# A two-layer encoder on one core: branch B's conversions get a higher priority, and GpSimd makes some low parts of the output weights

## The chip, the cores and the metric

The kernel runs on one core of a Trainium2 chip. A core has five engines with queues of their own: TensorE (PE, matrix multiplications into PSUM), VectorE (DVE), ScalarE (ACT), GpSimd (POOL) and SyncE (SP, which here issues every DMA). The metric is the device time of one execution in microseconds.

## The reference

Two layers act on x, 512 positions by 1024 features in float32. Each layer is a half-step SwiGLU FFN, a token mixing with two branches of heads, and a second half-step FFN; every sub-layer is RMS-normed and modulated by a shift, a scale and a gate that come from a conditioning vector. This change touches the mixing alone:

```python
def token_mixing(h, cos, sin, w_in, sink, onorm_a, onorm_b, w_out):
    proj = h @ w_in
    qa, ka, va, qb, kb, vb = jnp.split(proj, IN_SPLITS, axis=-1)
    ...
    oa, _ = banded_attention(qa, ka, va, A_HALF_WINDOW, sink)
    for window, dilation in B_BRANCHES:
        o, l = dilated_branch(qb, kb, vb, window, dilation)
        ...
    wts = jax.nn.softmax(jnp.stack(lses, axis=0), axis=0)
    ob = jnp.sum(wts[..., None] * jnp.stack(outs, axis=0).astype(jnp.float32), axis=0).astype(h.dtype)
    ya = rmsnorm(oa.reshape(b, s, A_WIDTH), onorm_a)
    yb = rmsnorm(ob.reshape(b, s, B_WIDTH), onorm_b)
    return jnp.concatenate([ya, yb], axis=-1) @ w_out
```

Both branches have eight query heads of 64 features; q and k are turned by rope first, and branch A's eight heads share two of k and v.

## The kernel before

Activations lie transposed, features on the 128 partitions and the 512 positions along a row. To keep float32's precision, a matrix product is made of three: each operand is split into a high part (a copy in TensorE's own float32 format) and a low part (what the copy left out), and `mm3` (L224) adds high x high (L226), high x the weight's low (L227) and low x high (L228) in PSUM.

Weights come in chunks of 128x1024. `emit_chunk` (L139) issues the DMA of one into a tile `raw` (L153); ScalarE copies it to `hi` (L157) and VectorE subtracts to get `lo` (L158). For chunks near a change of sub-layer (`finer`) both are done in two pieces of 512 columns. The list `specs` holds the chunks in the order of use; a mixer ends with eight of `w_out`, four for branch B's half of the features (`half` 1), then four for branch A's.

The mixer makes q, k and v, then sixteen heads, B's eight first. One head: scores on TensorE (L698, L699), the mask and the row's least value on VectorE (L703, reading PSUM), exp on ScalarE (L707), a transpose of the probabilities on TensorE (`ptr`, L732), their high part on ScalarE (`ph`, L735) and low part on VectorE (`pl`, L736), and the product with v (`po`, L739, L740). The `rope` of each q and k tile uses VectorE and, for one product and for the low part, GpSimd (L612, L616); its results are copied into place by DMAs that SP issues.

`weave` interleaves the heads with a filling stream: after each step of a head it adds the rate of `RATES` to a debt and emits fill until the debt is paid. The fill is first the remaining projections (`fill_b`), then branch B's part of the output projection (`fill_a`): eight output tiles of four `mm3`, 96 matmuls. For that B's eight heads are normed: `stat` and `bcast` (L778, L787) are hooked into the tenth and eleventh heads, `bcast` ends in the tile R (L794), and `conv` (L796) scales each of B's four tiles by R (L800), makes its high part `yh` (L801) and its low part `yl` (L802). After the last head the rest of the fill is emitted, with branch A's norm, then A's four conversions (`yah`, `yal`) and A's part of the projection.

The order on each engine is fixed when the kernel is built. A scheduler takes the emitted instructions by priority, which is the place of emission unless `high_priority(offset=...)` moves it forward. Heads of branch B stand HB = 50 forward, those of A HA = 150, branch A's norm and conversions HP = 300. Branch B's conversions stand where they are emitted.

Of the kernel before, what the change touches and what calls it, by code (L numbers as in the profile page):

```python
# [11 lines left out]
F32 = mybir.dt.float32  # L12
# [3 lines left out]
ALU = mybir.AluOpType  # L16
# [29 lines left out]
HP = 300  # L46
# [6 lines left out]
VK = ((0, 3), (3, 3), (6, 2))  # L53
PAIRS = ("b0", "b1", "b2", "b3", "a0", "a1", "a2", "a3")
HJ = [(9, 0), (10, 0)]
RATES = ((0, 2.2), (4, 1.0), (8, 0.65))
HL = 200
BY_POOL = (1, 3, 4, 6, 7)
AW = 1.5
# [9 lines left out]
def tile_trunk(ctx: ExitStack, tc: tile.TileContext, xT, c, positions, adaT, cols, sink, wi1, wo1,  # L69
# [38 lines left out]
    temps = [None, None]  # L108
    specs = []
    finer = set()  # L110
    live = {}
    state = {"emit": 0, "use": 0}

    for l in range(L):
        for sub, (wi, wo) in enumerate(((wi1, wo1), (None, None), (wi2, wo2))):
            finer.update(range(len(specs) - 3, len(specs) + 6))
            if wi is None:
                specs += [wqk[l, QK.index(t)] for t in FIRST]
                for t in FILL:
                    if t[0] == "v":  # L120
                        for k0, n in VK:
                            specs.append(wv[l, int(t[1])][:, k0 * 320:(k0 + n) * 320])
                    else:
                        specs.append(wqk[l, QK.index(t)])
                for half in (1, 0):
                    for m2 in range(4):
                        specs.append(w_out[l, half, m2])
            else:
                for f0, n in THIRDS:
                    for f in range(f0, f0 + n):  # L130
                        if paired(l, sub, f):
                            specs.append((wi[l, f, 0], wi[l, f, 1]))
                        else:
                            specs.append(wi[l, f, 0])
                            specs.append(wi[l, f, 1])
                    for m in range(KD):
                        specs.append(wo[l, m][:, f0 * 128:(f0 + n) * 128])

    def emit_chunk(pieces=1):  # L139
        i = state["emit"]  # L140
# [10 lines left out]
        hi = wp.tile([128, 1024], F32R, tag="hi", name="hi")  # L151
        lo = wp.tile([128, 1024], F32R, tag="lo", name="lo")
        nc.sync.dma_start(raw[:, :n], ap)  # L153
        step = 512 if i in finer else n
        for a in range(0, n, step):
            sl = slice(a, min(a + step, n))
            A.activation(hi[:, sl], raw[:, sl], AF.Copy)  # L157
            V.tensor_tensor(lo[:, sl], raw[:, sl], hi.bitcast(F32)[:, sl], op=ALU.subtract)  # L158
        live[i] = (hi, lo)

    def parts(t):
# [435 lines left out]
    def mixer(l, norm, pool, mod):  # L597
# [313 lines left out]
        def fill_a():  # L911
            while not hasattr(bb, "R"):
                yield None
            for ft in range(4):
                bb.conv(ft)
                yield FT
            for job in jobs():
                m, W, w0 = job()
# [273 lines left out]
```

## Time and profile before

| | us |
|---|---|
| median of 3 runs (lowest, highest) | 1941.79 (1940.43, 1943.55) |
| profiled execution | 1941.13 |
| span of its profile | 1939.4 |
| TensorE busy | 1903.8 (98%) |
| VectorE busy | 1516.0 (78%) |
| ScalarE busy | 941.6 (49%) |
| GpSimd busy | 85.5 (4%) |

The profile is one execution. The span runs from its first instruction to its last; the execution has 1.7 us around it. A matmul's duration overlaps the next one's, so TensorE can be busy and yet not at its pace; the number of matmuls in a stretch says more. The heads of the first mixer end shortly before 610 us of the span, those of the second shortly before 1550.

### The profile page before, as it was taken

The numbers are of one execution on the slowest core, as the hardware profiler recorded it, in microseconds if no ns is written. First come the engines' busy times: TensorE is split into PE (matmuls) and PEld (weight loads), VectorE is DVE, ScalarE is ACT, GpSimd is POOL, SyncE is SP. The second block draws the span as 40 slices with busy tenths as digits, with TensorE's granted clock in tenths as the row PEclk, the third lists the DMA queues.
The fourth block names the chain that finished last, engine by engine and source line by source line (L and its number), as shares of the span: only waits on it lengthen the run. The fifth ranks groups of instructions, "written<-read, shape, count | busy, mean of one in ns | idle before, by whom it ended". The sixth has DMA issues, their size and how long they took to land.

```text
span 1939.4 us, 30969 instructions
## 1 busy us (share of the span) xinstructions
PE 1903.8 (98%) x12000; PEld 1711.2 (88%) x12000; DVE 1516.0 (78%) x2653; ACT 941.6 (49%) x1782; POOL 85.5 (4%) x63
## 2 busy tenths in 40 slices
PE   7999999999999999999999999999999999999998
PEld 5788888898778999989999898999887799898998
DVE  8967484477888989899688898867778889686873
ACT  5422222246675554536445363644567656363552
POOL 2000000011210000000000000000211000000000
PEclk8999999999999999999999999999999999999999
DMA  8778384245422255464424545342543113233231
GB/s 298 282 255 308 126 304 137 76 129 139 118 55 66 77 164 195 142 209 129 142 66 152 196 144 161 109 131 83 153 116 99 44 57 111 86 106 123 87 110 44
DMA packets 84677, 267.95 MB, mean 138 GB/s; under 512 B 10673, under 2 KB 13361, under 8 KB 84530
## 3 DMA queue, kind: packets, MB, share of 16 engines
q1 hardware_dynamic: 84530, 265.98, 42.6%
q8 instruction: 94, 1.54, 0.3%
q14 instruction: 53, 0.43, 0.1%
HBM read 244.97 MB, written 2.10 MB: 127 GB/s over the span
## 4 chain that ended last, share of the span: by engine, by line
PE 90%; DVE 5%; ACT 2%; DMA 2%; issue 1%; SPq 0%; POOL 0%; DVEq 0%; ACTq 0%; POOLq 0%
PE mm L226 17%; PE mm L227 17%; PE mm L228 17%; PE mm L488 10%; PE mm L489 10%; PE mm L490 10%; PE ptr L732 2%; PE po L739 1%; PE po L740 1%; PE s L698 1%; PE s L699 1%; DVE araw L320 1%; DMA araw<-in_adaT_dram 1%; PE mm L661 1%; PE mm L663 1%
## 5 line engine op out<-in xcount | busy, mean ns | idle before, releaser
L157 ACT ACTIVATE hi<-raw 128x512 fp32r<-128x512 f32 (+5 forms) x253 | 215.7, 866 | 310.2 <-PE mm L228 224.2
L158 DVE TENSOR_TENSOR lo<-raw,hi 128x512 fp32r<-128x512 f32 (+5 forms) x253 | 259.2, 1037 | 88.6 <-ACT hi L157 87.6
L226 PE MATMUL mm<-hh,hi 128*128 128x512 f32 (+1 forms) x864 | 307.7, 357 | 6.9 <-ACT hh L298 6.6
L228 PE MATMUL mm<-hl,hi 128*128 128x512 f32 (+1 forms) x864 | 303.1, 355 | 2.8 <-DVE hl L299 2.8
L227 PE MATMUL mm<-hh,lo 128*128 128x512 f32 (+1 forms) x864 | 305.8, 355 | 0.0
L227 PE MATMUL mm<-gh,lo 128*128 128x512 f32 (+1 forms) x832 | 297.0, 357 | 0.0
L226 PE MATMUL mm<-gh,hi 128*128 128x512 f32 (+1 forms) x832 | 296.8, 357 | 0.0
L228 PE MATMUL mm<-gl,hi 128*128 128x512 f32 (+1 forms) x832 | 296.5, 356 | 0.0
L488 PE MATMUL mm<-sh,hi 128*128 128x256 f32 x912 | 260.0, 285 | 0.3 <-ACT sc L518 0.3
L489 PE MATMUL mm<-sh,lo 128*128 128x256 f32 x912 | 258.1, 283 | 0.0
L490 PE MATMUL mm<-sl,hi 128*128 128x256 f32 x912 | 258.0, 283 | 0.0
L185 ACT ACTIVATE hi<-raw 128x512 fp32r<-128x512 f32 x228 | 132.0, 623 | 140.3 <-issue 73.6
L396 DVE SCALAR_TENSOR_TENSOR x<-mm,fin,x 128x512 f32<-128x512 f32 (+1 forms) x156 | 101.4, 653 | 115.7 <-PE mm L228 115.2
L226 PEld LDWEIGHTS mm<-hh,hi 128*128 128x128 f32 x864 | 164.6, 191 | 29.7 <-ACT hh L298 8.1
L228 PEld LDWEIGHTS mm<-hl,hi 128*128 128x128 f32 x864 | 163.2, 190 | 25.9 <-DVE hl L299 4.7
L227 PEld LDWEIGHTS mm<-hh,lo 128*128 128x128 f32 x864 | 164.4, 190 | 20.7 <-DVE lo L1004 0.3
L228 PEld LDWEIGHTS mm<-gl,hi 128*128 128x128 f32 x832 | 157.2, 189 | 22.7
L227 PEld LDWEIGHTS mm<-gh,lo 128*128 128x128 f32 x832 | 157.2, 189 | 22.3
L226 PEld LDWEIGHTS mm<-gh,hi 128*128 128x128 f32 x832 | 157.2, 189 | 22.2
L488 PEld LDWEIGHTS mm<-sh,hi 128*128 128x128 f32 x912 | 174.0, 191 | 0.7 <-ACT sc L518 0.6
L489 PEld LDWEIGHTS mm<-sh,lo 128*128 128x128 f32 x912 | 174.2, 191 | 0.0
L490 PEld LDWEIGHTS mm<-sl,hi 128*128 128x128 f32 x912 | 174.1, 191 | 0.0
(185 smaller groups left out, 4017.1 us busy)
## 6 DMA issues: line engine op xcount, KB each, us to landing
raw<-in_wi_dram SPq DMA_DIRECT2D x171, 512.0 KB, 3.7
araw<-in_adaT_dram SPq DMA_DIRECT2D x144, 512.0 KB, 4.6
raw<-in_wo_dram SPq DMA_DIRECT2D x64, 448.0 KB, 3.8
raw<-in_wo_dram SPq DMA_DIRECT2D x32, 512.0 KB, 3.6
raw<-in_wqk_dram SPq DMA_DIRECT2D x26, 512.0 KB, 3.7
raw<-in_w_out_dram SPq DMA_DIRECT2D x16, 512.0 KB, 3.7
kh<-qh SPq DMA_DIRECT2D x40, 128.0 KB, 2.3
kl<-t SPq DMA_DIRECT2D x40, 128.0 KB, 2.3
```

What stands on the lines that cost most here:

```text
L157: A.activation(hi[:, sl], raw[:, sl], AF.Copy)
L158: V.tensor_tensor(lo[:, sl], raw[:, sl], hi.bitcast(F32)[:, sl], op=ALU.subtract)
L185: A.activation(d, r, AF.Copy)
L226: T.matmul(ps, wh, X[0][:, s], start=start, stop=False)
L227: T.matmul(ps, wl, X[0][:, s], start=False, stop=False)
L228: T.matmul(ps, wh, X[1][:, s], start=False, stop=stop)
L320: return V.tensor_tensor_reduce(out=raw, in0=raw, in1=by, scale=1.0, scalar=0.0, op0=ALU.mult, op1=ALU.add, accum_out=mod[:, l, ch, k:k + ...
L396: ins = V.scalar_tensor_tensor(x[:, m, s], ps[:, s], gate[:, m:m + 1], x[:, m, s], op0=ALU.mult, op1=ALU.add).ins
L488: T.matmul(ps, wh, xh, start=start and k == 0, stop=False, skip_group_check=True)
L489: T.matmul(ps, wl, xh, start=False, stop=False, skip_group_check=True)
L490: T.matmul(ps, wh, xl, start=False, stop=stop and k == 3, skip_group_check=True)
L732: T.transpose(p[:, j * 128:j * 128 + 128], self.sm[qt][:, c0:c0 + 128], ident)
```

## The change

Three things. The rate of filling from the ninth head on (branch A's heads) goes from 0.65 to 0.55. Four of each mixer's eight `w_out` chunks, the third to the sixth in the list, are split in pieces of 512, and their subtraction is issued on GpSimd in place of VectorE. And branch B's four conversions are emitted with the priority HP.

```diff
--- before.py
+++ after.py
@@ -53,7 +53,7 @@
 VK = ((0, 3), (3, 3), (6, 2))
 PAIRS = ("b0", "b1", "b2", "b3", "a0", "a1", "a2", "a3")
 HJ = [(9, 0), (10, 0)]
-RATES = ((0, 2.2), (4, 1.0), (8, 0.65))
+RATES = ((0, 2.2), (4, 1.0), (8, 0.55))
 HL = 200
 BY_POOL = (1, 3, 4, 6, 7)
 AW = 1.5
@@ -108,6 +108,7 @@
     temps = [None, None]
     specs = []
     finer = set()
+    by_pool = set()
     live = {}
     state = {"emit": 0, "use": 0}
 
@@ -124,6 +125,8 @@
                         specs.append(wqk[l, QK.index(t)])
                 for half in (1, 0):
                     for m2 in range(4):
+                        if m2 // 2 == half:
+                            by_pool.add(len(specs))
                         specs.append(w_out[l, half, m2])
             else:
                 for f0, n in THIRDS:
@@ -151,11 +154,11 @@
         hi = wp.tile([128, 1024], F32R, tag="hi", name="hi")
         lo = wp.tile([128, 1024], F32R, tag="lo", name="lo")
         nc.sync.dma_start(raw[:, :n], ap)
-        step = 512 if i in finer else n
+        step = 512 if i in finer or i in by_pool else n
         for a in range(0, n, step):
             sl = slice(a, min(a + step, n))
             A.activation(hi[:, sl], raw[:, sl], AF.Copy)
-            V.tensor_tensor(lo[:, sl], raw[:, sl], hi.bitcast(F32)[:, sl], op=ALU.subtract)
+            (G if i in by_pool else V).tensor_tensor(lo[:, sl], raw[:, sl], hi.bitcast(F32)[:, sl], op=ALU.subtract)
         live[i] = (hi, lo)
 
     def parts(t):
@@ -912,7 +915,8 @@
             while not hasattr(bb, "R"):
                 yield None
             for ft in range(4):
-                bb.conv(ft)
+                with tc.high_priority(offset=HP):
+                    bb.conv(ft)
                 yield FT
             for job in jobs():
                 m, W, w0 = job()
```

VectorE's order at branch B's conversions in the first mixer. Before (L715 and L716 make a head's denominator, L755 and L750 a head's result, L611 and L613 belong to a rope, L703 and L736 as above):

```order
L611 TENSOR_TENSOR t_4802<-mm,rc 128x512
L715 TENSOR_TENSOR den<-den,es 128x4
L800 SCALAR_TENSOR_TENSOR y<-y,col,R 128x512
L716 RECIPROCAL den<-den 128x4
L613 TENSOR_TENSOR t_4802<-t_4802,part 128x512
L800 SCALAR_TENSOR_TENSOR y<-y,col,R 128x512
L802 TENSOR_TENSOR yl<-y,yh 128x512
L736 TENSOR_TENSOR pl<-ptr,ph 128x384
L736 TENSOR_TENSOR pl<-ptr,ph 128x256
L802 TENSOR_TENSOR yl<-y,yh 128x512
L800 SCALAR_TENSOR_TENSOR y<-y,col,R 128x512
L750 TENSOR_TENSOR y<-po,y 64x512
```

And now, where L803 is the old L800, L805 the old L802, and L718, L758, L719, L739 and L706 the old L715, L755, L716, L736 and L703:

```order
L718 TENSOR_TENSOR den<-den,es 128x4
L758 TENSOR_TENSOR y<-y,pd 128x512
L803 SCALAR_TENSOR_TENSOR y<-y,col,R 128x512 x4
L805 TENSOR_TENSOR yl<-y,yh 128x512 x4
L719 RECIPROCAL den<-den 128x4
L739 TENSOR_TENSOR pl<-ptr,ph 128x384 x2
L706 ISA sm,nb<-s,mask,nsnk 128x384
L706 ISA nb 128x1
L739 TENSOR_TENSOR pl<-ptr,ph 128x256
```

Before, the four L800 stand at places 679, 682, 687 and 715 of VectorE's order, among the heads. Now the four stand together at 649, with the four subtractions behind them, and the next denominator and `pl` of the heads come after.

TensorE's order at the end of branch B's projection in the first mixer, where `pRo` are the transposes of branch A's norm, `yh` and `yl` branch B's parts and `yah` branch A's. Before:

```order
L227 MATMUL mm<-yh,lo 128x512
L228 MATMUL mm<-yl,hi 128x512
L790 MATMUL pRo<-ident,y_5537 128x128 x4
L226 MATMUL mm<-yah,hi 128x512
L227 MATMUL mm<-yah,lo 128x512
```

And now (L793 is the old L790, L229 to L231 the old L226 to L228):

```order
L229 MATMUL mm<-yh,hi 128x512
L793 MATMUL pRo<-ident,y_5516 128x128 x4
L230 MATMUL mm<-yh,lo 128x512
L231 MATMUL mm<-yl,hi 128x512
L229 MATMUL mm<-yh,hi 128x512
```

Before, the first `yah` matmul follows `pRo`; now 17 matmuls of branch B, of which three are seen here, stand between.

GpSimd's order in the first mixer, at the ropes of branch A's q tiles (`t_...` is the low part of one). Before:

```order
L612 TENSOR_TENSOR part<-part,rs 128x512
L616 TENSOR_TENSOR t_4393<-t_4393,qh 128x512
L612 TENSOR_TENSOR part<-part,rs 128x512
L616 TENSOR_TENSOR t_4520<-t_4520,qh 128x512
L612 TENSOR_TENSOR part<-part,rs 128x512
L616 TENSOR_TENSOR t_4642<-t_4642,qh 128x512
```

And now (L615 and L619 are the old L612 and L616):

```order
L615 TENSOR_TENSOR part<-part,rs 128x512
L161 TENSOR_TENSOR lo<-raw,hi 128x512 x2
L619 TENSOR_TENSOR t_4393<-t_4393,qh 128x512
L161 TENSOR_TENSOR lo<-raw,hi 128x512
L615 TENSOR_TENSOR part<-part,rs 128x512
L161 TENSOR_TENSOR lo<-raw,hi 128x512
L619 TENSOR_TENSOR t_4520<-t_4520,qh 128x512
L161 TENSOR_TENSOR lo<-raw,hi 128x512
L615 TENSOR_TENSOR part<-part,rs 128x512
L161 TENSOR_TENSOR lo<-raw,hi 128x512
L619 TENSOR_TENSOR t_4642<-t_4642,qh 128x512
L161 TENSOR_TENSOR lo<-raw,hi 128x512 x2
```

The eight `lo` of the four chunks stand between the instructions of these ropes, four of them between a rope's product and its low part.

## Rows read from the trace of the kernel before

**Rows 1.** The page: busy time of the engines, and the chain that ended last.

```profile
PE 1903.8 (98%) x12000; PEld 1711.2 (88%) x12000; DVE 1516.0 (78%) x2653; ACT 941.6 (49%) x1782; POOL 85.5 (4%) x63
...
PE 90%; DVE 5%; ACT 2%; DMA 2%; issue 1%; SPq 0%; POOL 0%; DVEq 0%; ACTq 0%; POOLq 0%
```

**Rows 2.** Windows: stretch, length, busy us (instructions) per engine, TensorE clock, DMA share, GB/s.

```profile
100.00:200.00 100.00, 100.00 (x443) 82.82 (x442) 68.02 (x100) 26.91 (x32) 0.00 (x0) 1.00 0.75 267
560.00:570.00 10.00, 7.08 (x32) 4.80 (x32) 9.34 (x28) 8.85 (x27) 1.27 (x1) 0.80 0.00 1
570.00:580.00 10.00, 9.94 (x50) 8.30 (x50) 8.26 (x20) 6.26 (x16) 1.67 (x1) 0.86 0.24 55
580.00:590.00 10.00, 10.00 (x56) 8.49 (x55) 9.25 (x26) 7.85 (x24) 0.00 (x0) 1.00 0.10 33
590.00:600.00 10.00, 9.63 (x56) 8.07 (x56) 8.97 (x22) 7.43 (x19) 0.00 (x0) 1.00 0.06 22
610.00:620.00 10.00, 8.28 (x42) 6.68 (x41) 8.38 (x19) 3.68 (x6) 0.00 (x0) 1.00 0.26 77
1500.00:1510.00 10.00, 7.71 (x38) 5.30 (x37) 9.33 (x29) 9.61 (x30) 1.26 (x1) 0.90 0.00 0
1510.00:1520.00 10.00, 9.01 (x41) 7.21 (x42) 8.68 (x19) 6.23 (x14) 1.66 (x1) 0.76 0.23 54
1550.00:1560.00 10.00, 8.24 (x44) 6.46 (x43) 8.80 (x20) 4.30 (x7) 0.00 (x0) 1.00 0.23 76
```

**Rows 3.** Timeline, R to `yh`: start, us, instruction, [idle before <- what ended it].

```profile
557.53 0.58 ACT L794 ACTIVATE R<-pRo 128x512 f32<-128x512 f32 x1
...
568.23 0.75 DVE L800 SCALAR_TENSOR_TENSOR y<-y,col,R 128x512 f32<-128x512 f32 x1
...
569.01 0.63 ACT L801 ACTIVATE yh<-y 128x512 fp32r<-128x512 f32 x1 [0.43 <-DVE y L800]
...
569.70 0.80 PE L226 MATMUL mm<-yh,hi 128*128 128x512 f32 x1 [0.99 <-ACT yh L801]
```

**Rows 4.** Windows from R to the first `yh` matmul, both mixers.

```profile
558.40:569.70 11.30, 8.02 (x38) 5.32 (x36) 10.64 (x34) 10.15 (x32) 1.27 (x1) 0.83 0.00 1
1500.00:1511.50 11.50, 8.47 (x39) 5.55 (x37) 10.83 (x33) 10.40 (x32) 1.26 (x1) 0.85 0.00 0
```

**Rows 5.** Timeline of VectorE: low parts of the four chunks.

```profile
526.28 1.22 DVE L158 TENSOR_TENSOR lo<-raw,hi 128x1024 fp32r<-128x1024 f32 x1
...
531.51 2.04 DVE L158 TENSOR_TENSOR lo<-raw,hi 128x1024 fp32r<-128x1024 f32 x1
...
549.71 1.79 DVE L158 TENSOR_TENSOR lo<-raw,hi 128x1024 fp32r<-128x1024 f32 x1
...
585.94 0.68 DVE L158 TENSOR_TENSOR lo<-raw,hi 128x512 fp32r<-128x512 f32 x1
```

**Rows 6.** Timeline of TensorE at the change from branch B to A.

```profile
611.39 0.60 PE L790 MATMUL pRo<-ident,y 128*128 128x128 f32 x4
...
613.71 0.50 PE L226 MATMUL mm<-yah,hi 128*128 128x512 f32 x1 [1.72 <-ACT yah L801]
```

**Rows 7.** Lines of GpSimd by form: us busy, mean ns of one | idle before.

```profile
L616 POOL TENSOR_TENSOR t<-t,qh 128x512 f32<-128x512 f32 x26 | 37.5, 1441 | 89.2 <-ACT qh L614 89.2
L612 POOL TENSOR_TENSOR part<-part,rs 128x512 f32<-128x512 f32 x26 | 35.5, 1367 | 1302.8 <-DVE part L610 1302.8
```

**Rows 8.** Timeline where GpSimd meets VectorE.

```profile
545.18 1.30 POOL L612 TENSOR_TENSOR part<-part,rs 128x512 f32<-128x512 f32 x1 [9.00 <-DVE part L610]
...
545.53 0.67 DVE L755 TENSOR_TENSOR y<-y,pd 128x512 f32<-128x512 f32 x1
...
562.78 1.27 POOL L612 TENSOR_TENSOR part<-part,rs 128x512 f32<-128x512 f32 x1 [12.37 <-DVE part L610]
...
562.86 1.21 DVE L715 TENSOR_TENSOR den<-den,es 128x4 f32<-128x4 f32 x1
...
568.16 0.15 DVE L715 TENSOR_TENSOR den<-den,es 128x4 f32<-128x4 f32 x1
```

## The prediction

> **What bounds the kernel now.** I read the page first: TensorE is busy for 1903.8 of 1939.4 us and makes up 90% of the chain that ended last, while VectorE is busy for 1516.0 us [rows 1]. So a microsecond counts only where TensorE stands still or is granted a lower clock, and the windows of 10 us say where that is. In layer 0's mixer it is 560 to 570 us (TensorE 7.08 us busy, clock 0.80), 570 to 580 (clock 0.86) and 610 to 620 (8.28 busy); layer 1 repeats it at 1500 to 1520 and 1550 to 1560 [rows 2]. In those windows VectorE has its highest shares, 8.3 to 9.3 us of 10. The reader is to see there that the mixer's end is the one stage in which VectorE, not TensorE, sets the pace, for about 45 us a layer.
>
> The timeline says why. Branch B's broadcast norm R is copied at 557.53 us, but the first conversion L800, which needs nothing else, starts at 568.23, since the heads of branch A have a higher priority in VectorE's order. yh follows at 569.01, and TensorE's first matmul of B's output projection at 569.70, waiting for it [rows 3]. From 558.4 to 569.7 TensorE has only the A heads and runs 38 matmuls in 11.3 us [rows 4]. From 580 to 590, where it is never idle, 56 take 10 us, 0.179 us each [rows 2]; 38 would take 6.8 us, so 4.5 us are lost, a part of it by the clock of 0.83 in that stretch.
>
> **The change part by part.**
>
> *Priority of the four conversions.* They leave their places among the heads in VectorE's order and enter in one block: four L800, then four L802, right behind R. No instruction is added. With R done at 558.1, four L800 of 0.75 us [rows 3] end near 561.4, and four L802, taken at the 0.68 of a subtraction of that size [rows 5], near 564.1. ScalarE's first yh (0.63 us) can be done near 559.8 instead of 569.64 and the first yl at 562.1. What waits is the A heads' softmax: TensorE's order holds 20 matmuls between R and the first po that needs a pl from behind the block, and that pl comes at about 564.9 (reciprocal and one L736 more). 20 x 0.179 = 3.6 us of work in 6.5 us: 2.9 us lost instead of 4.5. The hole is not closed, it is made smaller and moved. What is won beyond it is that most of the 96 matmuls of B's projection (88 behind the first eight) lie ready from 565 us on, to fill the A heads' waits, instead of from 570.
>
> *The clock.* In 570 to 580 TensorE was 9.94 us busy at a granted 0.86: with the levels 1.2 and 2.4 GHz that is 28% of the window at half speed, 1.4 us lost. It fell after the stretch in which TensorE stood still by turns. In the changed order that stretch is 6.5 us long instead of 11.3. Bounds: the fall stays (0 gained) or goes (1.4 gained). I take half, 0.7 us.
>
> *The lower rate of filling (0.65 to 0.55 from the ninth head on).* It leaves matmuls of B's projection for the end. Before, none stands between the transposes pRo of branch A's norm (from 611.39) and the first yah matmul at 613.71, which waits 1.72 us for the conversions [rows 6]. Now 17 stand there. At 443 matmuls of 512 columns in 100 us [rows 2] they take 3.8 us, more than the 2.3 us from pRo to yah. The hidden wait is worth 1.7 us. What is late next is the fill missing among the A heads: 17 matmuls less to cover VectorE's chains. Bounds 0 and 3.8 us given back; between 580 and 600 TensorE is 9.6 to 10 us busy with VectorE near 9 [rows 2], so the two are nearly in balance, and I take 1.0.
>
> *GpSimd's low parts.* Per layer four chunks go from VectorE to GpSimd, as eight instructions of 128x512. VectorE loses three of 128x1024 (1.22, 2.04 and 1.79 us) and two of 128x512 (0.68 each): 6.4 us [rows 5]. The first two lie where TensorE is hardly ever idle and give nothing. The third stands inside the chain that makes R's root, and its 1.8 us delay that chain, whose transposes then come behind other TensorE work: bounds 0 and 1.8, taken as 0.4. The pair of 0.68 stands among the A heads, in the 45 us that VectorE paces: bounds 0 and 1.4, taken as 0.8. GpSimd needs 1.37 to 1.44 us for 128x512 [rows 7], so eight take 11 us of an engine that is busy 1.3 us in those 11.3 [rows 4]. ScalarE's three hi parts of 1024 become six of 512; it is 90% busy in the stretch behind R [rows 4], but these six come before it, so I count nothing. GpSimd's order now has these low parts in front of the rope's own low parts, and the copies of q issued by SP wait for those. At most two of 1.4 us stand ahead of one, so q comes up to 2.9 us later. The projections are filled in ahead of the heads that need them, which hides it; if that cover were gone, it would cost up to 2.9 us for each of the four q tiles of branch A. I count nothing.
>
> *What GpSimd does to VectorE.* Here a row speaks against the change. VectorE's L715, 128x4 from two inputs in SBUF, takes 1.21 us at 562.86, just behind the start of a GpSimd multiplication at 562.78; at 568.16, with GpSimd idle, it takes 0.15. L755, with one input in PSUM, takes 0.67 us in the middle of another [rows 8], and the 128x1024 subtractions take 1.79 and 2.04 beside GpSimd against 1.22 alone [rows 5]. So an instruction with two SBUF inputs stands until GpSimd is through, one that reads PSUM does not. The Trainium skill (SBUF — State Buffer, section Who interferes with whom) says the same as a rule: the pair of ports is an exclusive lock, and whoever comes second blocks wholly. By that rule a move to GpSimd gives VectorE less than it takes off; the trace agrees, with 1.21 us against 0.15. Most softmax instructions read PSUM. The fourth chunk's pair, though, comes due on GpSimd right behind the four yh, while L802 (two SBUF inputs) runs: bounds 0 and 2 x 1.4 us. I take 0.7.
>
> **The sum, per layer:** hole 4.5 - 2.9 = 1.6; clock 0.7; tail 1.7; less fill -1.0; low parts 0.4 + 0.8; lock -0.7. That is 3.5 us, and 7.0 for both layers, since layer 1 shows the same pattern: 39 matmuls in the 11.5 us from 1500 [rows 4], clock 0.90 and 0.76, and 8.24 busy in 1550 to 1560 [rows 2]. The profiled execution took 1941.13 us; 1934.1 remain. The median of the runs is 1941.79, 0.66 more, so I give 1934.8, said as 1935.
>
> **The rivals.**
>
> *VectorE paces the stretch anyway.* The conversions are only moved. If VectorE's work between 558 and 605 is the bound, the A heads end as late as before, and only the fourth chunk's pair (1.4 us per layer) comes off; the tail's 1.7 us is then paid among the heads by the missing fill. For it: 8.3 to 9.3 us busy in each window. Against: its idle time in 560 to 600 is still 4.2 us [rows 2], much of it waits for a TensorE at half clock. Result 2 x 1.4 = 2.8 us, 1939: no measurable change.
>
> *TensorE becomes the bound.* With the fill early and the clock whole, only the hole of 2.9 stays: 4.5 + 1.4 + 1.7 - 2.9 + 1.4 + 0.4 = 6.5 per layer, 13 in all, 1929. For it: before, windows with the fill present (580 to 590) have TensorE at 10.00. Against: VectorE at 9.25 in that same window leaves little room.
>
> *GpSimd's lock (the slower side).* Sixteen low parts, each able to hold a two-input instruction for about 1.05 us (1.21 less 0.15 [rows 8]). If all sixteen hit VectorE's path, 16.8 us are lost against the 7.0 + 1.4 gained otherwise (the 0.7 per layer is already in the sum): 1941.8 - 8.4 + 16.8 = 1950. It is slower by more than 0.2% from about 12 hits on the path. For it: the two rows of collisions. Against: six of eight per layer fall before 558 us, where TensorE has fill to go on with, so a held VectorE is hidden.
>
> *The change does less than it says.* If yh waited for the tiles it overwrites, the hh of the last projection, the block would stand in VectorE's queue before all heads. The order has the last hh matmuls ahead of the first yh by seven places, so this would be 1 us or so, and it lies inside the other cases.
>
> **How the numbers follow.** My forecast 0.47 (1931 to 1938 as its own range), TensorE the bound 0.17, VectorE paces anyway 0.25, the lock 0.11. About 0.2% (3.9 us) is what a measurement of this kernel can tell from no change. Faster than 1937.9: 0.43 of the forecast's 0.47, all of the second, 0.04 of the third: 0.64. Within: 0.04 + 0.21 + 0.03 = 0.28. Slower: 0.08. The range reaches from just under TensorE's bound of 1929 to 1943, somewhat above the time before, for the smaller part of the lock's cases.
>
> **What would show it.** After: L803 right behind R (within 1 us), first yh matmul about 2 us behind R instead of 12; a TensorE wait of 2 to 3 us for yl or pl in that place; the wait for yah gone or under 0.3 us; VectorE's low parts fewer by 6.4 us per layer and GpSimd busy 20 us more; windows of the A heads with TensorE at 9.5 or more. I am wrong if the first yh matmul comes early and the last yah matmul of the mixer does not come at least 2 us earlier, or if the second pass, L805, or L718 (the old L715) often shows durations over 1.2 us: then the lock, or VectorE, has taken it back.

## The result, and the profile after

The changed kernel takes 1953.68 us (median of 4 runs, 1951.44 to 1954.96), the kernel before on the same chip 1942.28 (4 runs, 1940.43 to 1943.55): a ratio of 1.0054, with a 95% interval of 1.0039 to 1.0069. By that ratio it is slower by 10.5 us, where 7 us less were forecast. The rival that forecast slower, the port that GpSimd and VectorE share, had a chance of 0.11 and nearly the right size (1950 us), but as the runs show, not the right cause. Single executions far off the others (2060, 2906 and 4208 us in three of the variants below, 3106 in the kernel before) are left out of the ratios, though not of the medians.

The page of the changed kernel, busy time and the chain that ended last:

```profile
PE 1911.2 (98%) x12000; PEld 1714.3 (88%) x12000; DVE 1510.4 (77%) x2643; ACT 942.8 (48%) x1788; POOL 107.5 (6%) x79
...
PE 88%; DVE 5%; ACT 2%; DMA 2%; issue 1%; POOL 1%; SPq 0%; DVEq 0%; POOLq 0%; ACTq 0%
```

Set beside [rows 1], GpSimd is busy 22 us more, as forecast, but VectorE only 5.6 us less, not the 12.8 of its low parts. TensorE's share of the chain fell from 90% to 88% and GpSimd, which had 0%, has 1%: an engine that is busy 6% of the span has come onto the path.

**Where the time went.** Three points of the mixer's timeline separate its parts: the first pd matmul of the mixer, the copy of R, and the first and last matmul of branch A's projection (yah). From the first pd matmul (462.53 us before, 462.87 after) to R, which came at 557.53 [rows 3], it took 95.0 us and now takes 102.8 in the mixer of layer 0, and 95.0 against 102.7 in that of layer 1. From R to the first yah matmul it took 56.2 and 56.3 us, and now 55.0 and 53.8; the yah matmuls save another 0.5. So the end of the mixer, of which the prediction spoke, did become shorter by 1.7 and 3.0 us, and 7.7 us were lost ahead of it in each mixer, in a part that the prediction had passed over. (These parts make 10.7 us. The two profiled executions, 1954.96 and 1941.13, are 13.8 apart; the other 3 us lie outside the mixers' ends, and no run here explains them.) The copy of R in the changed kernel's timeline (columns as in [rows 3]), and behind it the conversions, the first yh matmul, and the change from branch B to branch A:

```profile
565.62 0.58 ACT L797 ACTIVATE R<-pRo 128x512 f32<-128x512 f32 x1
...
566.43 2.73 DVE L803 SCALAR_TENSOR_TENSOR y<-y,col,R 128x512 f32<-128x512 f32 x4
569.08 2.49 DVE L805 TENSOR_TENSOR yl<-y,yh 128x512 fp32r<-128x512 f32 x4
...
568.02 0.50 PE L229 MATMUL mm<-yh,hi 128*128 128x512 f32 x1 [0.94 <-ACT yh L804]
...
569.82 0.51 PE L231 MATMUL mm<-yl,hi 128*128 128x512 f32 x1 [1.07 <-DVE yl L805]
...
620.36 0.39 PE L231 MATMUL mm<-yl,hi 128*128 128x512 f32 x1
620.59 0.39 PE L229 MATMUL mm<-yah,hi 128*128 128x512 f32 x1
```

The conversions stand behind R in one block, yh's first matmul comes 2.4 us behind R instead of 12.2 [rows 3], and the 1.72 us of waiting for yah [rows 6] are gone. That much came as predicted.

Ahead of R it is another kernel. Windows of 5 us of the changed kernel (columns as in [rows 2]):

```profile
525.00:530.00 5.00, 3.78 (x17) 2.52 (x16) 3.13 (x9) 3.88 (x9) 0.93 (x1) 1.00 0.73 209
530.00:535.00 5.00, 4.51 (x25) 3.81 (x26) 2.40 (x6) 2.86 (x7) 1.43 (x2) 1.00 0.00 1
535.00:540.00 5.00, 2.56 (x15) 1.89 (x14) 3.76 (x6) 0.94 (x3) 3.61 (x3) 1.00 0.30 101
540.00:545.00 5.00, 5.00 (x23) 4.10 (x21) 2.89 (x10) 3.05 (x9) 0.00 (x0) 0.66 0.37 109
...
555.00:560.00 5.00, 3.44 (x23) 2.80 (x24) 3.51 (x7) 1.24 (x3) 1.35 (x1) 1.00 0.70 210
```

TensorE is busy 3.78, 2.56 and 3.44 us of 5 in three of these windows. Before, it was busy 5.00 us in every window of 5 us from 520 to 560 but two (4.56 each), always at a clock of 1.00. Behind the emptiest one the granted clock is 0.66 for 5 us, a mean between the levels of 2.4 and 1.2 GHz. VectorE, at 2.4 to 3.8 us of 5 in these windows, is not short of time here. What TensorE waited for from 520 to 560 us, changed kernel (total us, times, longest):

```profile
PE po L743 <- DVE pl L739: 3.4, 2, 2.4
PE s L701 <- DMA qs<-t: 1.4, 1, 1.4
PE pso L785 <- DVE acco L779: 0.8, 1, 0.8
```

With one more of 0.3 us, on VectorE's L706, these are all; the second mixer has the same list, with 1.2 in place of 1.4. Before, the same list held two waits of 0.4 us. TensorE thus stands still some 5.1 us longer, and at a clock of 0.66 for 5 us it loses 1.7 more: 6.8 of the 7.7 us. The engine behind most of these waits is GpSimd. Its timeline in the changed kernel, over the ropes of the first two q tiles of branch A:

```profile
520.00 1.29 POOL L615 TENSOR_TENSOR part<-part,rs 128x512 f32<-128x512 f32 x1 [6.64 <-DVE part L613]
521.25 2.99 POOL L161 TENSOR_TENSOR lo<-raw,hi 128x512 fp32r<-128x512 f32 x2
524.20 1.73 POOL L619 TENSOR_TENSOR t<-t,qh 128x512 f32<-128x512 f32 x1
533.57 1.29 POOL L161 TENSOR_TENSOR lo<-raw,hi 128x512 fp32r<-128x512 f32 x1 [7.64 <-ACT hi L160]
534.82 1.28 POOL L615 TENSOR_TENSOR part<-part,rs 128x512 f32<-128x512 f32 x1
536.06 1.26 POOL L161 TENSOR_TENSOR lo<-raw,hi 128x512 fp32r<-128x512 f32 x1
538.61 1.29 POOL L619 TENSOR_TENSOR t<-t,qh 128x512 f32<-128x512 f32 x1 [1.28 <-ACT qh L617]
```

In the first rope two low parts stand in front of L619, which makes q's low part. It starts at 524.20, against 523.11 before; 0.33 of that the kernel had lost already at the shuffle, and a part is VectorE's L616, which took 1.37 us beside a low part instead of 0.69. More is added on the way. SP, which issues every DMA, has the load of a later weight chunk in front of q's copies, and that load waits for the chunk buffer which the low part on GpSimd frees at 524.24. SP in the changed kernel, and the time from issue to landing of the last two copies, changed and before:

```profile
524.27 0.33 SPq L156 DMA_DIRECT2D raw<-in_w_out_dram  x1
...
525.96 0.48 SPq L627 DMA_DIRECT2D qs<-t  x1
...
qs<-t SPq DMA_DIRECT2D x2, 128.0 KB, 4.3
```

```profile
qs<-t SPq DMA_DIRECT2D x2, 128.0 KB, 2.3
```

Before, VectorE's low part freed the buffer later and the load went out at 527.52, behind the copies. Now the copies are issued behind it, the last at 526.49, and take 4.3 us to land instead of 2.3. TensorE waits for them until 530.49, the 1.4 us of the list. At 2.3 us the last would have landed by 528.8, before TensorE came to it at 529.06 (an estimate from these rows). So this wait is not the order of GpSimd's queue alone: a low part that ended earlier let a load go ahead of the copies, and behind it they landed later. That the load is the whole reason is not shown: in the second mixer of the kernel before, two such copies took 4.1 and 3.9 us with no load right in front.

In the second rope a low part stands in front of L615, the product, and another one behind it. VectorE at that rope, in the changed kernel and, with GpSimd's product, before:

```profile
532.87 0.74 DVE L613 STREAM_SHUFFLE part<-mm 128x512 f32<-128x512 f32 x1
533.50 0.67 DVE L614 TENSOR_TENSOR t<-mm,rc 128x512 f32<-128x512 f32 x1
536.14 1.73 DVE L616 TENSOR_TENSOR t<-t,part 128x512 f32<-128x512 f32 x1 [1.96 <-POOL part L615]
537.79 1.28 DVE L739 TENSOR_TENSOR pl<-ptr,ph 128x512 fp32r<-128x512 f32 x2
```

```profile
530.29 0.74 DVE L610 STREAM_SHUFFLE part<-mm 128x512 f32<-128x512 f32 x1
...
531.17 1.30 POOL L612 TENSOR_TENSOR part<-part,rs 128x512 f32<-128x512 f32 x1 [6.46 <-DVE part L610]
...
533.47 0.68 DVE L613 TENSOR_TENSOR t<-t,part 128x512 f32<-128x512 f32 x1
534.08 1.28 DVE L736 TENSOR_TENSOR pl<-ptr,ph 128x512 fp32r<-128x512 f32 x2
```

L616 waits 1.96 us for the product, then meets the second low part and takes 1.73 us instead of 0.68. The subtraction that makes pl, which TensorE needs, is queued behind it. TensorE, changed kernel:

```profile
535.70 0.40 PE L229 MATMUL mm<-hh,hi 128*128 128x512 f32 x1
538.53 0.50 PE L743 MATMUL po<-pl,v 128*128 128x512 f32 x1 [2.44 <-DVE pl L739]
```

In the second rope and the third the two meet, and not by chance. ScalarE's hi for this chunk and VectorE's shuffle for the rope are released by one event, the end of the projection's last L231 matmuls, which frees the weight buffer and hands the rope its input (changed kernel, ScalarE and VectorE):

```profile
532.86 1.15 ACT L160 ACTIVATE hi<-raw 128x512 fp32r<-128x512 f32 x2 [0.49 <-PE mm L231]
...
532.87 0.01 DVE L613 LOAD_MASK_SELECT part<-mm  x1 [0.53 <-PE mm L231]
```

The low part and the product thus become due within 0.2 us of each other (the first hi takes 0.6 us, the shuffle 0.74), and GpSimd's order has the low part first. In the third rope it is the same: hi at 550.33, shuffle at 550.34, and there L616 waits 0.58 us for the product and takes 1.77. The last wait of the list, 0.8 us for acco, stands behind VectorE's L779, which takes 1.78 us beside that rope's L619.

### The profile page after: what moved, and what is told of

Same layout as the page of the kernel before. It is cut to its first block, busy times and chain, and to the rows that moved or that the text cites. A ratio compares the mean times of both kernels' runs of the same rounds, so it can differ in the third digit from the quotient of the medians.

```text
span 1953.2 us, 30975 instructions
## 1 busy us (share of the span) xinstructions
PE 1911.2 (98%) x12000; PEld 1714.3 (88%) x12000; DVE 1510.4 (77%) x2643; ACT 942.8 (48%) x1788; POOL 107.5 (6%) x79
## 4 chain that ended last, share of the span: by engine, by line
PE 88%; DVE 5%; ACT 2%; DMA 2%; issue 1%; POOL 1%; SPq 0%; DVEq 0%; POOLq 0%; ACTq 0%
PE mm L231 17%; PE mm L230 17%; PE mm L229 17%; PE mm L491 10%; PE mm L492 9%; PE mm L493 9%; PE ptr L735 2%; PE po L742 1%; PE po L743 1%; PE s L701 1%; PE s L702 1%; PE mm L664 1%; PE mm L666 1%; PE mm L665 1%; DVE araw L323 1%
## 5 line engine op out<-in xcount | busy, mean ns | idle before, releaser
L160 ACT ACTIVATE hi<-raw 128x512 fp32r<-128x512 f32 (+4 forms) x259 | 216.1, 850 | 296.7 <-PE mm L231 210.0
L229 PE MATMUL mm<-hh,hi 128*128 128x512 f32 (+1 forms) x864 | 308.8, 358 | 8.0 <-ACT hh L301 8.0
L161 DVE TENSOR_TENSOR lo<-raw,hi 128x512 fp32r<-128x512 f32 (+5 forms) x243 | 246.3, 1024 | 88.8 <-ACT hi L160 88.3
L231 PE MATMUL mm<-hl,hi 128*128 128x512 f32 (+1 forms) x864 | 305.0, 358 | 2.4 <-DVE hl L302 2.4
L229 PE MATMUL mm<-gh,hi 128*128 128x512 f32 (+1 forms) x832 | 296.8, 357 | 0.0
L231 PE MATMUL mm<-gl,hi 128*128 128x512 f32 (+1 forms) x832 | 296.5, 356 | 0.0
L229 PEld LDWEIGHTS mm<-hh,hi 128*128 128x128 f32 x864 | 165.3, 191 | 31.3 <-ACT hh L301 10.1
L231 PEld LDWEIGHTS mm<-hl,hi 128*128 128x128 f32 x864 | 164.2, 191 | 25.1 <-DVE hl L302 3.8
L231 PEld LDWEIGHTS mm<-gl,hi 128*128 128x128 f32 x832 | 157.2, 189 | 22.6
L229 PEld LDWEIGHTS mm<-gh,hi 128*128 128x128 f32 x832 | 157.2, 189 | 22.3
```

Of the source, the lines that this page charges most:

```text
L161: (G if i in by_pool else V).tensor_tensor(lo[:, sl], raw[:, sl], hi.bitcast(F32)[:, sl], op=ALU.subtract)
L229: T.matmul(ps, wh, X[0][:, s], start=start, stop=False)
L231: T.matmul(ps, wh, X[1][:, s], start=False, stop=stop)
```

## The experiments

Two theories on the loss ahead of R were to be told apart. **Q**: what costs is the order of GpSimd's queue, with low parts standing in front of the ropes' instructions. **L**: what costs is the port of SBUF that both engines use, wherever the low parts run. Beside them stood doubts on the other two parts of the change. All times are medians of 5 to 12 executions (4 of the changed kernel); the ratio is to runs of the kernel before on the same chip, and the last column is that ratio (and its 95% interval) times 1941.7 us, less 1941.7. Variants were measured on three chips, so they are compared by their ratios.

| kernel | us | ratio [95%] | against before, us |
|---|---|---|---|
| changed kernel | 1953.7 | 1.0054 [1.0039, 1.0069] | +10.5 (+7.6 to +13.4) |
| low parts on VectorE | 1938.8 | 0.9984 [0.9975, 0.9993] | -3.1 (-4.9 to -1.4) |
| low parts on GpSimd alone | 1953.9 | 1.0069 [1.0056, 1.0083] | +13.4 (+10.9 to +16.1) |
| conversions' priority alone | 1946.7 | 1.0023 [1.0012, 1.0034] | +4.5 (+2.3 to +6.6) |
| changed, qa ropes on VectorE | 1941.7 | 0.9997 [0.9988, 1.0006] | -0.6 (-2.3 to +1.2) |
| unit 0.55 alone | 1938.9 | 0.9980 [0.9971, 0.9989] | -3.9 (-5.6 to -2.1) |
| changed, low parts behind the ropes | 1939.0 | 0.9984 [0.9975, 0.9992] | -3.1 (-4.9 to -1.6) |
| changed, last two chunks on GpSimd | 1937.2 | 0.9969 [0.9957, 0.9981] | -6.0 (-8.3 to -3.7) |
| changed, qa ropes and low parts on VectorE | 1940.8 | 0.9994 [0.9986, 1.0003] | -1.2 (-2.7 to +0.6) |
| unit 0.55 and last two chunks | 1937.4 | 0.9973 [0.9964, 0.9983] | -5.2 (-7.0 to -3.3) |
| last two chunks, unit 0.50 | 1941.1 | 0.9993 [0.9984, 1.0002] | -1.4 (-3.1 to +0.4) |
| changed, one chunk on GpSimd | 1942.7 | 1.0002 [0.9994, 1.0011] | +0.4 (-1.2 to +2.1) |

### The parts one by one

**Low parts back on VectorE.**

```diff
-            (G if i in by_pool else V).tensor_tensor(lo[:, sl], raw[:, sl], ...)
+            V.tensor_tensor(lo[:, sl], raw[:, sl], ...)
```

> The changed kernel with the eight low parts of each mixer back on VectorE (their halves of 512, the conversions' priority and the unit of 0.55 stay). Theory Q (GpSimd's in-order queue): all of the loss is the low parts that wait for ScalarE's copies in front of the ropes' instructions, about 7.5 to 8 us per mixer before R; without them R is back at 557.5 +-1.5 us (before 557.53, changed 565.62), and only the gain of the conversions is left, which the changed kernel's trace puts at 1.7 us per mixer from R to the tail: 1939 (1937 to 1941). Theory L (lock of the SBUF port between VectorE and GpSimd, whatever the queue's order): the same, 1939, since no low part is on GpSimd. Rival U (the unit of 0.55 moves the projections into worse places, and GpSimd is innocent): 1950 or more, R still near 565. Rival C (the conversions' priority loses more than it gives): above 1943 with R at 557.5.

This is the changed kernel otherwise. 1938.8 us, and the stretch from the first pd matmul to R is 95.6 us in both mixers (95.0 before, 102.8 and 102.7 changed). Of TensorE's waits from 500 to 562 us one of 0.5 is left. So the low parts on GpSimd cost 13.6 us, some 3 either way (1.0054 less 0.9984 of 1941.7), and the rest of the change gains 3.

**Low parts on GpSimd alone.** The changed kernel without its other two parts:

```diff
-RATES = ((0, 2.2), (4, 1.0), (8, 0.55))
+RATES = ((0, 2.2), (4, 1.0), (8, 0.65))
-                with tc.high_priority(offset=HP):
-                    bb.conv(ft)
+                bb.conv(ft)
```

> The kernel before with the eight low parts on GpSimd and nothing else (conversions at the branch norm's order, unit 0.65). Theories Q and L: before plus the whole loss ahead of R without the conversions' gain: 1942 + 2 x 7.5 to 8 = 1957 to 1958 (1954 to 1960), R near 565, and VectorE's product sum of the rope held by a GpSimd product behind a low part. Rival U: 1942 to 1944, R at 557.5.

1953.9 us, 13.4 more than before: the same price from the other side, somewhat under the expected 15 to 16. Its waits ahead of R repeat those of the changed kernel to a tenth (pl 3.4, qs 1.4, acco 0.8), and R comes 101.2 and 102.0 us behind the first pd matmul.

**Conversions' priority alone.** The kernel before, with only this:

```diff
             for ft in range(4):
-                bb.conv(ft)
+                with tc.high_priority(offset=HP):
+                    bb.conv(ft)
                 yield FT
```

> The kernel before with the conversions' priority and nothing else (unit 0.65, no split, low parts on VectorE). Theories Q and L: 1939 (1937 to 1941), as the variant that has the unit of 0.55 beside it; the wait of 1.7 us in front of the last output chunks stays unless the unit takes it away, so it may keep 1 us per mixer of it: 1939 to 1941. Rival C: 1943 or more. Were the conversions worth the 2.3 us per mixer that the prediction gave them: 1937 to 1938.

A miss: it is slower than before by 4.5 us. R comes no later (95.0 and 95.1 us behind the first pd matmul), but the stretch from R to the first yah matmul takes 56.7 and 57.0 us instead of 56.2 and 56.3. The fill starts 10 us earlier and, at the old rate, is used up earlier. TensorE's timeline in this kernel, at the end of branch B:

```profile
608.65 0.39 PE L228 MATMUL mm<-yl,hi 128*128 128x512 f32 x1
608.88 1.00 PE L782 MATMUL pso<-ones,sqo 128*128 128x1 f32 x8
612.58 1.09 PE L790 MATMUL pRo<-ident,y 128*128 128x128 f32 x4 [2.69 <-DVE y L243]
615.16 0.79 PE L226 MATMUL mm<-yah,hi 128*128 128x512 f32 x1 [1.50 <-ACT yah L801]
```

Between the last yl matmul and the first yah matmul 6.5 us pass with nothing but the branch norm, and the window from 600 to 620 has a clock of 0.83. Behind it the yah part of the projection takes 26.2 and 26.8 us instead of 24.3, which is most of the loss. What the conversions win in front they lose at the back.

**Unit 0.55 alone.** The kernel before, with only this:

```diff
-RATES = ((0, 2.2), (4, 1.0), (8, 0.65))
+RATES = ((0, 2.2), (4, 1.0), (8, 0.55))
```

> The kernel before with the unit 0.55 in place of 0.65 and nothing else. The two runs before this one disagree on the conversions: with the unit they gained (1938.8), without it they lost (1946.7, with 6.7 us between the last yh matmul and the first yah matmul instead of 2.8). Theory T (the fill runs dry at the end of the mixer; the unit stretches it, the conversions' priority only starts it earlier): the unit alone takes most of the 2.8 us away and leaves the hole behind R, so 2 x 1.7 us less, R about 0.6 us later: 1939 to 1941. Rival S (the unit is worth nothing by itself, the two gain only together): 1942 to 1944. Rival W (the unit alone holds the whole gain of the pair): 1938 to 1939.

1938.9 us, a ratio of 0.9980, which is all that the pair gains (0.9984). The rival W holds. R still is followed by yh only after 11.7 and 11.4 us, and the hole behind R is as it was. TensorE in this kernel at the end of branch B:

```profile
614.27 0.39 PE L228 MATMUL mm<-yl,hi 128*128 128x512 f32 x1
614.50 0.39 PE L226 MATMUL mm<-yah,hi 128*128 128x512 f32 x1
```

What the trace shows gone is the wait of 1.72 us at the end: yah follows yl without a gap.

### Queue or port

**The ropes of qa on VectorE**, so that GpSimd has nothing that others wait for, while the eight low parts stay on it:

```diff
-            G.tensor_tensor(part, part, rs, op=ALU.mult)
+            E = V if kind[:2] == "qa" else G
+            E.tensor_tensor(part, part, rs, op=ALU.mult)
...
-            G.tensor_tensor(t1, t1, qh, op=ALU.subtract)
+            E.tensor_tensor(t1, t1, qh, op=ALU.subtract)
```

> The changed kernel with the product and the low part of the four qa ropes of each mixer moved from GpSimd to VectorE, so that on GpSimd nothing that others wait for stands behind a low part; the eight low parts stay on GpSimd and still share the port with VectorE. Theory Q: the waits for q's copies (1.4 us), for the rope's product (2.0 us) and for pl behind it (2.4 and 0.9 us) go, and VectorE pays some 8 x 0.7 us more per mixer in a stretch where it isn't the bound: R near 558 to 560, 1939 to 1944. Theory L: eight low parts of 1.3 us still stretch what VectorE has beside them by about 1 us each, so 4 to 7 of the 7.5 us per mixer stay: 1948 to 1954.

1941.7 us: some 11 of the 13.6 us are back, with all eight low parts still on GpSimd and VectorE busier than in the changed kernel (1514.0 us against 1510.4). Of TensorE's waits ahead of R (500 to 562 us) 1.4 us are left. The port is still met, and at the same ropes: VectorE's sum of the rope takes 1.24 us at 523.16 and 1.18 at 535.06, its product 1.05 at 533.49 and 1.18 at 548.64, beside low parts, where 0.68 is usual. R comes 96.6 and 97.5 us behind the first pd matmul all the same, not 102.7.

**Low parts behind the ropes.** Nothing is moved to another engine; only an order edge is added, so that GpSimd takes each low part behind the last rope written before it:

```diff
+    roped = [None]
...
+            with tc.issue_after(roped[0]) if i in by_pool else nullcontext():
+                (G if i in by_pool else V).tensor_tensor(lo[:, sl], raw[:, sl], ...)
...
-            G.tensor_tensor(t1, t1, qh, op=ALU.subtract)
+            roped[0] = G.tensor_tensor(t1, t1, qh, op=ALU.subtract).ins
```

> The changed kernel with one order edge more: GpSimd takes each low part behind the last rope low part written before it in the program, which puts all eight of a mixer behind the rope of qa3. Nothing is removed and no engine gets more work. Theory Q (the order of GpSimd's queue): the waits for q's copies, for the rope's product and for pl go, R is back at 558 to 560, 1939 to 1943; the eight low parts then run in one row of 11 us beside the output chunks of branch B, where a matmul may wait for one. Theory L (the port, whatever the order): the same eight meet other VectorE work there, which is at its busiest: 1948 to 1954.

1939.0 us, the whole 13.6 back by order alone. GpSimd's timeline in this kernel:

```profile
531.39 1.29 POOL L617 TENSOR_TENSOR part<-part,rs 128x512 f32<-128x512 f32 x1 [6.74 <-DVE part L615]
534.14 1.29 POOL L621 TENSOR_TENSOR t<-t,qh 128x512 f32<-128x512 f32 x1 [1.47 <-ACT qh L619]
...
584.18 1.30 POOL L621 TENSOR_TENSOR t<-t,qh 128x512 f32<-128x512 f32 x1 [10.09 <-ACT qh L619]
585.43 10.45 POOL L163 TENSOR_TENSOR lo<-raw,hi 128x512 fp32r<-128x512 f32 x8
```

The ropes run as they did before, and the eight low parts follow in one row. VectorE, in the same kernel beside that row, still shows the port:

```profile
582.69 0.17 DVE L720 TENSOR_TENSOR den<-den,es 128x4 f32<-128x4 f32 x1
...
590.94 1.30 DVE L781 TENSOR_TENSOR acco<-acco,sqo 128x512 f32<-128x512 f32 x1
...
593.89 0.76 DVE L720 TENSOR_TENSOR den<-den,es 128x4 f32<-128x4 f32 x1
```

The 128x4 instruction takes 0.76 us beside a low part and 0.17 just before them. So meetings happen and cost 0.6 us each on VectorE, but none of it reaches the time here. Theory L, by which the low parts cost the same wherever they run, is out. The edge moves more than the queue, though: with it no weight load goes out between 517 and 587 us, and q's copies in the first mixer land in 2.2 to 2.4 us again.

**Qa ropes and low parts on VectorE**, the run with the qa ropes on VectorE, where VectorE now makes the low parts too:

```diff
-            (G if i in by_pool else V).tensor_tensor(lo[:, sl], raw[:, sl], ...)
+            V.tensor_tensor(lo[:, sl], raw[:, sl], ...)
```

> The changed kernel with the low parts and the qa ropes' two GpSimd instructions both on VectorE, so that GpSimd does nothing in the second half of a mixer. Beside the run that had the qa ropes on VectorE and the low parts on GpSimd (1941.7) and the one with the ropes on GpSimd and the low parts on VectorE (1938.8) it tells what the 3 us between them are. If they are the port shared with eight low parts: 1938 to 1939.5. If they are VectorE's eight more instructions per mixer in the ropes: 1941 to 1943, or more, as VectorE has the low parts too.

1940.8 us. Against the kernel with only the low parts on VectorE it is 1.9 us more (0.9994 against 0.9984, intervals that overlap), in the sense of the ropes' eight instructions per mixer: R comes 96.5 and 96.4 us behind the first pd matmul, against 95.6. Against the kernel that has the low parts on GpSimd it is 0.6 us less (0.9994 against 0.9997), and the intervals overlap widely: with the queue free, sharing the port with eight low parts per mixer costs nothing that could be measured.

**One chunk on GpSimd.**

```diff
-                        if m2 // 2 == half:
+                        if half == 1 and m2 == 3:
```

> The changed kernel with one chunk's two low parts per mixer on GpSimd instead of four chunks' eight: the fourth chunk, whose first low part stands in front of the product of the rope of qa1 and whose second stands between that product and the rope's low part. Theory Q (what counts is what stands behind a waiting low part): the trace of the changed kernel puts 2.0 us of VectorE's wait for the product, 1.05 us of its stretch and 2.4 us of TensorE's wait for pl behind it at this chunk alone, so 2.4 to 4 us of the 7.7 us per mixer: 1943.5 to 1947. Rival P (the loss goes with the number of low parts on GpSimd): a quarter of 15 us: 1942.5; theory L as well, or less. If the waits of a single chunk have slack: 1939 to 1940.

1942.7 us, 3.5 more than with no low part on GpSimd (1.0002 less 0.9984), 1.7 per mixer, where 2.4 to 4 were expected. By time alone it can't be told from a loss that goes with the number of low parts. Its trace repeats the event: from 520 to 600 us VectorE's L616 waits 2.0 us for the product, takes 1.73 us, and TensorE waits 2.4 us for pl, though the load in front of the first rope's copies is back behind them. R comes 98.5 and 97.0 us behind the first pd matmul, against 95.6 with no low part on GpSimd, and from R to the first yah matmul it is 0.6 and 0.7 us shorter than there.

**The last two chunks on GpSimd** in place of the four in the middle:

```diff
-                        if m2 // 2 == half:
+                        if half == 0 and m2 >= 2:
```

> The changed kernel with other chunks on GpSimd: the last two of a mixer (four low parts of 512), which stand in GpSimd's queue behind the last rope. Theory Q: nothing is held, the conversions' gain stays: 1938 to 1941, R 558 to 560. Theory L: four low parts stretch four VectorE instructions by some 1 us each after R, where VectorE is at 0.9: 1943 to 1946. If VectorE's load after R sets the time, its relief of 4 x 0.68 us per mixer brings 1935 to 1937.

1937.2 us, the lowest median: four low parts per mixer on GpSimd, and faster than before. That the low parts add to what the unit gives is not shown (0.9969 against 0.9980, intervals that overlap). GpSimd in this kernel:

```profile
581.36 1.29 POOL L619 TENSOR_TENSOR t<-t,qh 128x512 f32<-128x512 f32 x1 [10.13 <-ACT qh L617]
582.61 2.99 POOL L161 TENSOR_TENSOR lo<-raw,hi 128x512 fp32r<-128x512 f32 x2
```

They come behind the last rope, and no rope's instruction stands behind them.

**The same without the conversions' priority**, and **the same with a unit of 0.50**:

```diff
-                with tc.high_priority(offset=HP):
-                    bb.conv(ft)
+                bb.conv(ft)
```

> The kernel before with the unit 0.55 and the last two chunks' low parts on GpSimd behind the last rope, without the conversions' priority: the run of 1937.2 less the conversions. Theory N (the conversions' priority only exchanges one work of TensorE for another and is worth nothing): 1937 to 1938.5, as with it. Rival G (the conversions gain once VectorE has some relief): 1939 to 1940.

```diff
-RATES = ((0, 2.2), (4, 1.0), (8, 0.55))
+RATES = ((0, 2.2), (4, 1.0), (8, 0.5))
```

> The run of 1937.2 (conversions first, last two chunks on GpSimd) with the unit at 0.50 in place of 0.55. Theory T (the unit only has to keep fill for the end of the heads): the wait in front of the first yah matmul is already 0.5 us, so a smaller unit gives nothing: 1936.5 to 1938.5, with somewhat more left over behind the heads. Rival M (each step of the unit puts work into holes): 1934 to 1936. One low part comes in front of the low part of the rope of qa3 in GpSimd's queue here; by theory Q it costs up to 1.4 us per mixer where q waits for it: up to 1940.

1937.4 us without the priority: a second pair of kernels (0.9973 and 0.9969, beside 0.9980 and 0.9984) in which the conversions are worth nothing that could be measured. With 0.50 it is 1941.1, slower than all three theories had it. The windows of that kernel, and of the one with 0.55, from 15 to 25 us behind R, show a part of it:

```profile
571.80:581.80 10.00, 8.40 (x50) 6.45 (x49) 9.32 (x28) 7.62 (x24) 1.29 (x1) 1.00 0.01 2
```

```profile
571.24:581.24 10.00, 9.91 (x60) 8.17 (x59) 9.15 (x26) 9.06 (x26) 0.00 (x0) 1.00 0.00 0
```

With 0.50 (first row) TensorE stands still for 1.6 us of these 10, with 0.55 (second row) for 0.1, and in the second mixer it is the same (8.40 and 9.92 us busy). This is what too little fill among the A heads would do. From R to the first yah matmul it takes 56.8 and 55.4 us with 0.50, 52.4 and 53.6 with 0.55, and no wait in front of yah is left in either. In the first mixer a clock of 0.77 in the 15 us behind R, where the run with 0.55 had 1.00, adds to it; in the second mixer both had 0.89. The first low part of that kernel on GpSimd starts at 581.97, behind these windows, so the queue has no part in what is lost there.

## Why the prediction was wrong

**The step that failed.** The low parts' row of the sum, 0.4 + 0.8 gained and 0.7 lost to the lock, made +0.5 us per layer. Measured, it is -6.7 to -6.8 (13.4 and 13.6 us for both layers, in two comparisons). In the working it is this passage: "The projections are filled in ahead of the heads that need them, which hides it; if that cover were gone, it would cost up to 2.9 us for each of the four q tiles of branch A. I count nothing." The order of GpSimd was read rightly, the price for the cover's failing was written down with its bound, and the cover was believed without a look at the rows of that stretch. It was thin: copies that were issued about 1 us late and landed 2 us slower had TensorE waiting until 530.49. The slower landing stands nowhere in the prediction, which followed GpSimd's order but not what a low part's end sets free: the next weight load, now in front of the copies. The prediction's own sign of being wrong came: the first yh matmul came early, and the first mixer's last matmul 6.4 us later, where it was to come at least 2 us earlier.

**What the step did not see at all.** It followed only the rope's low part, which q's copies wait for. The rope's product is behind a low part as well, VectorE waits for it in its own order, and pl, on which TensorE waits, stands behind that wait. The trace of before has the place: GpSimd's L612 for that rope ran at 531.17, and a low part on VectorE of 2.04 us, at 531.51 [rows 5], lay over the wait for it. From shuffle to pl VectorE took 3.79 us with the low part (530.29 to 534.08); in the changed kernel it takes 4.92 without it (532.87 to 537.79). The work taken off the busy engine had been the cover of the wait.

**"The first two lie where TensorE is hardly ever idle and give nothing."** Right as to the gain. But that VectorE's relief is worth nothing in a stretch says that a delay there may cost much: TensorE, never idle, has no slack to take it from. The windows chosen for the sum began at 558 us, and the loss ahead of R lies between 520 and 560.

**GpSimd's lock.** The rows show it: L616 1.73 us in the changed kernel against 0.68 before, the 128x4 instruction 0.76 against 0.17 with the low parts behind the ropes. The Trainium skill (SBUF — State Buffer, section Who interferes with whom) has the port pair as an exclusive lock, and these stretches agree. But with the low parts behind the ropes it costs nothing that can be measured, and where the prediction looked for it, at the four L805 behind R, they take 2.49 us together, 0.62 each, though a low part started at 570.64: the 0.7 per layer was too much there, and the rival that bore its name was slower for another reason. The stretches of L616 (0.7, 1.05 and 1.1 us in the three ropes) do stand in the chains to TensorE, beside the 1.96 and 0.58 us of waiting for the product and the slower copies. They come from one order of the queue and went together in the runs. With the qa ropes on VectorE stretches of 0.4 to 0.6 us at the same ropes brought R only 0.1 and 1.0 us later than without any (96.6 and 97.5 against 96.5 and 96.4), so the port alone is not the loss; how the 13.6 us divide between the queue, the port and the copies stays open. That moving the qa ropes to VectorE gives 11 of them and the order edge all is, for the most part, the price of the eight extra instructions (1.9 us).

**Hole and clock, 1.6 + 0.7.** Measured: nothing beyond the intervals of some 2 us either way (0.9984 against 0.9980, and 0.9969 against 0.9973), and at the old unit a loss of 4.5. That yh comes 2.4 us behind R was right, and so was a new wait for yl (1.07 and 0.80 us). The hole was only exchanged: what TensorE does early from branch B's projection it lacks among the A heads, where VectorE is as busy as it was. Between 30 and 35 us behind R TensorE is 4.0 us of 5 busy in both mixers of the changed kernel, 5.0 before and 4.8 and 4.9 with the unit alone. The clock did not follow the conversions either: over the 24 us behind R it was 0.86 in both mixers before, 0.86 and 0.93 in the changed kernel, 0.86 and 1.00 with the unit alone, each in one profiled execution. The rival that VectorE paces the stretch anyway described this part.

**The tail, 1.7 less 1.0.** Too small. The unit alone gains 3.9 us (2.1 to 5.6), 1.9 per layer, and the fill that was to be missing (1.0) isn't missed at 0.55; at 0.50 it is.

## What to carry to other kernels

Before work is moved to an engine that is nearly idle, read its queue in order: an engine that is busy 4% of the span can still be the one that another engine's next instruction waits for, and its 4% may be all hand-offs in the middle of a chain. Put the moved work behind the last of these hand-offs: here, with the last two chunks or an order edge, it cost nothing that could be measured. Look also at what the end of the moved work sets free: a buffer that comes free earlier can start a load in front of a transfer that somebody needs. When work is taken off a busy engine, look at what it was lying over; and where an early start of the fill looks like a gain, look at where the fill then ends.

## What the runs showed of the hardware that was not expected

GpSimd kept to its order in these rows: the product at 534.82 was due when the shuffle ended at 533.61 and ran only behind the low part. The Trainium skill (Perfetto Trace Analysis, section Tensor Engine Instruction (MATMUL, LD_WEIGHTS)) says in passing that GpSimd's FIFO is strict, and these rows agree.

The port holds GpSimd as well as VectorE. Where VectorE's L779 (two inputs in SBUF) ran from 523.61, GpSimd's L619 that started at 524.20 took 1.73 us; one of the eight low parts in a row, beside VectorE's 1.30 us of acco, took 1.74, and the row 10.45. A rope's instruction of that size takes 1.29 or 1.30 alone. VectorE's two-input instructions beside low parts took 0.4 to 1.1 us more.

A wait of 2.4 us can cost more than itself: in the window behind it TensorE ran 5 us at a mean granted clock of 0.66, which at the levels of 2.4 and 1.2 GHz is 68% of that window at the lower one, or 1.7 us more. It need not: in the second mixer of the kernel with one chunk on GpSimd the same wait (2.56 us busy of 5 there too) left the clock at 1.00, and R came 1.5 us sooner behind the first pd matmul than in the first mixer.
